# Attention scores of a head pair in two 64-row tiles of the array with three products, and probability transposes in halves of 64 queries

## The chip, the cores and the metric

The kernel runs on one core of a Trainium2 chip. The core has a matrix engine (TensorE, "PE" in the profile; its weight loads are listed apart as "PEld"), a vector engine (DVE), an activation engine (ACT), GpSimd (POOL), and a sync engine (SP) that here only issues transfers. Each engine takes its own queue of instructions in order; engines wait for one another through semaphores. Matrix results land in PSUM, where the kernel holds eight tiles ("banks") of 128 partitions by 512 fp32 numbers; all other on-chip data lies in SBUF. The metric is the device time of one execution in microseconds (us), the median of several runs.

A matrix instruction has a stationary operand, which is loaded into the array first (a weight load), and a moving operand, which is streamed through. The contraction runs over the partitions (the array's rows), and the columns of the stationary operand become the partitions of the result.

## The reference, cut to what matters

Two sequences (2048 and 512 tokens, 1024 channels, fp32) pass through an attention layer, a Fourier layer and a last norm. The change lies in the attention layer alone: 16 heads of 64 channels, 4 key/value heads, blocks of 128 queries that see three blocks of keys, an additive bias by distance, and a sink logit per head.

```python
h = rmsnorm(x, g)
z = h @ w_in                       # q, k, v, gate
scores = jnp.einsum('bnqhgd,bnkhd->bnhgqk', qb, kw).astype(jnp.float32) * scale + bias
scores = jnp.where(mask[None, :, None, None, :, :], scores, -jnp.inf)
m = jnp.maximum(jnp.max(scores, axis=-1, keepdims=True), sk)
p = jnp.exp(scores - m)
denom = jnp.sum(p, axis=-1, keepdims=True) + jnp.exp(sk - m)
p = p / denom
o = jnp.einsum('bnhgqk,bnkhd->bnqhgd', p, vw.astype(jnp.float32))
return x + (o * jax.nn.silu(gate)) @ w_out
```

## The kernel before

**Number format.** Products are made in `float32r`. Every operand is kept as two parts, `hi` (the number rounded to that type) and `lo` (the rest, made by DVE or POOL as number minus `hi`), and a product is the sum of hi·hi, hi·lo and lo·hi (`matmul3`, lines 93 to 97).

**Stages.** `attention_phase` goes through five chunks of 512 tokens (`CHUNKS`; chunk 0 is the short sequence, chunks 1 to 4 the long one). Each chunk projects keys and values (`kv_proj`), then runs 8 head pairs `p`, each with 4 query blocks `b` of 128 and 2 heads `j`. `fourier_phase` follows and is not touched.

**The loop.** For each chunk a loop over `i` (from 0 to 63 and a few more for the tail, line 712) has one (block, head) per step: `p, n = divmod(i, 8)`. A step traces, in this order: the scores of (b, j) (`at[p][1]`, line 742); the transposes of the probabilities that were scored `LAG` = 3 steps before (`at[..][2]`); half of this step's share of `fill`; every second step the product with the values, `av`, of the block whose transposes are `AVLAG` = 2 steps old, and after an odd block its `out_evac`; then the other half of `fill`. `fill` is the projection of the next head pair's queries and gates (`qg_proj`: 8 steps of three 512-column matmuls for q, an evacuation, the same for the gates), and for the last pair the output projection (`out_proj`), whose first half holds four PSUM banks at once (line 517).

**Scores (line 428).** `evac_q` (lines 370 to 378) writes, for each head, an operand of 128 rows: for head 0, `qa` has its 64 channels' hi in rows 0 to 63 (ACT, line 374) and their lo in rows 64 to 127 (DVE, line 375); for head 1, `qb` has hi in rows 64 to 127 (lines 376, 377) and lo in rows 0 to 63. The keys `kwin[g]` hold the same 64 channels twice, in rows 0 to 63 and again in rows 64 to 127, hi in part 0 and lo in part 1. So two matmuls of 128 rows per head, one with the keys' hi and one with their lo, give all four products. They go into one of two PSUM tiles `spt`, in turn. The moving operand has 384 columns (three blocks of keys), or 256 at either end of a sequence.

**Softmax.** On `S` (five buffers, `LAG + 2`): DVE adds the bias and takes the extremum (line 440), ACT takes the exponential and its sum (444), DVE the reciprocal (447) and the scaling (450; for chunk 0 and odd heads ACT, 453).

**Transposes (line 467).** Per (b, j) one transpose for each of the two or three blocks of keys; S is the stationary operand (128 queries by 128 keys), the identity the moving one (128 columns). The results of one head share a PSUM bank from the pool of six (`bank`); ACT writes hi (468) and DVE lo (469) into `pts`.

**Values (line 481).** Per block up to six matmuls of 256 columns (both heads side by side).

**Order.** The framework's scheduler places instructions by the order in which they are traced and by when its own model holds them ready; `tc.keep_in_program_order` pins an instruction behind all that was traced before it on its engine.

Of the kernel before, what the change touches and what calls it, by code (L numbers as in the profile page):

```python
# [18 lines left out]
P = 128  # L19
# [9 lines left out]
LAG = 3  # L29
AVLAG = 2  # L30
BIG = 1.0e30
LINE = 512
# [7 lines left out]
def f32(ap):  # L40
    return ap.bitcast(F32)
# [3 lines left out]
def encoder(  # L45
# [13 lines left out]
    ident = cpool.tile([P, P], F32, name="ident")  # L59
# [18 lines left out]
    def bank(name):  # L78
        return psum.tile([P, 512], F32, tag="bank", name=name)
# [55 lines left out]
    def attention_phase():  # L135

        with ExitStack() as es:
# [216 lines left out]
            def qg_proj(c, p, hs, res, invb=None):  # L354
# [15 lines left out]
                def evac_q():  # L370
                    ps = scaled(st["psq"], invb, f"q{p}")
                    qab = ap.tile([P, 2, CH], F32R, align_bytes=LINE, tag="qab", bufs=2, name=f"qab{c}_{p}")
                    qa, qb = qab[:, 0], qab[:, 1]
                    ACT.activation(qa[0:64], ps[0:64], AF.Copy, scale=-0.125)
                    DVE.scalar_tensor_tensor(qa[64:128], ps[0:64], -0.125, f32(qa[0:64]), ALU.mult, ALU.subtract)
                    ACT.activation(qb[64:128], ps[64:128], AF.Copy, scale=-0.125)
                    DVE.scalar_tensor_tensor(qb[0:64], ps[64:128], -0.125, f32(qb[64:128]), ALU.mult, ALU.subtract)  # L377
                    res["q"] = (qa, qb)
# [18 lines left out]
            def attention(c, p, res, uTs):  # L397
# [24 lines left out]
                def scores(b, j):  # L422
                    gb, k0, k1 = span(b)
                    q = res["q"][j][:, b * P : (b + 1) * P]
                    ps = spt[nS[0] % 2]
                    nS[0] += 1
                    for part in range(2):
                        PE.matmul(  # L428
                            ps[:, 2 + k0 * P : 2 + k1 * P],
                            q,  # L430
                            kwin[g][:, part, b * P + k0 * P : b * P + k1 * P],
                            start=part == 0,
                            stop=part == 1,
                        )
# [3 lines left out]
                    s = ap.tile([P, 388], F32, tag="S", bufs=LAG + 2, name=f"S{c}_{p}_{b}_{j}")  # L438
# [20 lines left out]
                def transp(b, j):  # L459
                    gb, k0, k1 = span(b)  # L460
                    s = st.pop((b, j))
                    if j == 0:
                        st["pt", b] = ap.tile([P, 2, 3, 2, P], F32R, align_bytes=LINE, tag="pt", bufs=2, name=f"pts{c}_{p}_{b}")
                    hi, lo = (st["pt", b][:, i] for i in range(2))
                    ps = bank(f"pt{c}_{p}_{b}_{j}").rearrange("p (k q) -> p k q", q=P)
                    for kb in range(k0, k1):
                        PE.transpose(ps[:, kb, :], s[:, 1 + kb * P : 1 + (kb + 1) * P], ident)  # L467
                    ACT.copy(hi[:, k0:k1, j, :], ps[:, k0:k1, :])  # L468
                    DVE.tensor_tensor(lo[:, k0:k1, j, :], ps[:, k0:k1, :], f32(hi[:, k0:k1, j, :]), ALU.subtract)  # L469
# [214 lines left out]
            HB = [(b, j) for b in range(4) for j in range(2)]  # L684
# [7 lines left out]
            for c in range(len(CHUNKS)):  # L692
# [19 lines left out]
                for i in range(64 + LAG + AVLAG):  # L712
# [851 lines left out]
```

## Time and profile before

| | |
|---|---|
| median of 3 runs | 1649.08 us (1646.85 to 1652.1) |
| the profiled execution's own time | 1648.75 us |
| its span from the first to the last instruction | 1647.0 us |
| mean granted TensorE clock | 0.998 |
| busy: PE, PEld, DVE, ACT, POOL | 99%, 85%, 73%, 54%, 26% |
| first and last score matmul (line 428) | 48.0 and 1071.8 us from the start of the span |
| score matmuls, transposes, value matmuls | 640, 896, 896 |

How to read it: the page and its views come from one profiled execution. In a timeline row the columns are the start in us, the length in us, the engine, the line of the kernel, the operation, what is written and read, and how many were merged into the row. The ends of matmuls are modelled, and neighbours overlap in the record: what a matmul occupies the array for is read from the starts of neighbours, not from the length. In a view of groups the columns are the line, engine, operation and form, the count, then the sum in us and the mean in ns, then idle time of that engine just before. A row of the view of stretches gives the stretch, its length, and for each engine its busy time and count of instructions.

### The profile page before, as it was taken

How to read it: one execution, taken by the hardware profiler on the slowest of the kernel's cores; microseconds unless marked ns; L12 is line 12 of the kernel's file. 1: busy time of each engine (PE TensorE's matmuls, PEld its weight loads, DVE VectorE, ACT ScalarE, POOL GpSimd, SP SyncE). 2: the span in 40 equal slices, each digit the busy share in tenths (PEclk: the TensorE clock that was granted, in tenths of full speed). 3: DMA queues.
4: the chain of work that ended last, by engine and by line, in shares of the span. 5: the costliest groups of instructions: out<-in, count | busy, mean ns of one | idle time of the engine just before them, and what ended most of it. 6: DMA issues, size and time to landing. Idle time of an engine off the chain costs nothing.

```text
span 1647.0 us, 25858 instructions
## 1 busy us (share of the span) xinstructions
PE 1628.4 (99%) x8939; PEld 1401.4 (85%) x8939; DVE 1199.0 (73%) x2844; ACT 892.7 (54%) x2035; POOL 434.5 (26%) x605
## 2 busy tenths in 40 slices
PE   9999999999999999999999999999999999999998
PEld 7887888888898888988888888888888888888886
DVE  6787565888538886478884588858767667988696
ACT  6788644677326675256762466636545454343252
POOL 2454751431404322224214142121111111100010
PEclk9999999999999999999999999999999999999999
DMA  8475886665766555765648765657565469655862
GB/s 303 150 284 213 314 319 225 221 230 186 278 218 227 196 217 182 279 250 160 233 140 312 252 210 187 217 195 249 205 237 185 173 220 391 217 192 191 333 208 90
DMA packets 100637, 374.05 MB, mean 227 GB/s; under 512 B 12139, under 2 KB 22379, under 8 KB 83100
## 3 DMA queue, kind: packets, MB, share of 16 engines
q1 hardware_dynamic: 81708, 297.91, 52.2%
q0 software_dynamic: 16464, 70.30, 11.0%
q10 hardware_dynamic: 2336, 4.20, 0.7%
q8 instruction: 71, 1.16, 0.3%
q14 instruction: 58, 0.48, 0.1%
HBM read 281.10 MB, written 91.26 MB: 226 GB/s over the span
## 4 chain that ended last, share of the span: by engine, by line
PE 82%; DMA 4%; DVE 4%; POOL 3%; ACT 3%; issue 2%; SPq 0%; POOLq 0%; DVEq 0%; ACTq 0%
PE av L481 6%; PE spt L428 6%; PE pt L467 5%; PE qp L95 4%; PE qp L97 4%; PE qp L96 4%; PE op L95 4%; PE gp L95 4%; PE op L97 4%; PE gp L97 4%; PE op L96 4%; PE gp L96 4%; PE W L96 2%; PE W L97 2%; PE W L95 2%
## 5 line engine op out<-in xcount | busy, mean ns | idle before, releaser
L444 ACT ACTIVATE S<-S 128x385 f32<-128x385 f32 (+1 forms) x320 | 190.8, 596 | 63.3 <-DVE S L440 61.5
L469 DVE TENSOR_TENSOR pts<-pt,pts 128x384 fp32r<-128x384 f32 (+1 forms) x320 | 168.4, 526 | 42.0 <-ACT pts L468 39.6
L468 ACT CAST pts<-pt 128x384 fp32r<-128x384 f32 (+1 forms) x320 | 144.0, 452 | 83.4 <-PE pt L467 80.3
L440 DVE CUSTOM_DVE_ANT_0 S<-spt,b 128x385 f32<-128x385 f32 (+1 forms) x320 | 168.4, 527 | 28.2 <-PE spt L428 25.7
L428 PE MATMUL spt<-kwin,qab 128*128 128x384 f32 (+1 forms) x640 | 157.2, 327 | 1.9 <-DVE S L440 1.7
L500 POOL TENSOR_TENSOR o<-o,s 128x256 f32<-128x256 f32 x75 | 55.3, 738 | 375.0 <-DVE o L498 374.9
L467 PE MATMUL pt<-ident,S 128*128 128x128 f32 x896 | 150.7, 273 | 0.0
L428 PEld LDWEIGHTS spt<-kwin,qab 128*128 128x128 f32 x640 | 117.9, 188 | 27.9 <-DVE S L440 3.0
L95 PE MATMUL qp<-h,wq 128*128 128x512 f32 x320 | 137.5, 430 | 2.0 <-ACT wq L116 1.4
L95 PE MATMUL gp<-h,wg 128*128 128x512 f32 x320 | 137.8, 431 | 0.0
L481 PEld LDWEIGHTS av<-pts,v 128*128 128x128 f32 x896 | 126.3, 189 | 12.1 <-DVE qab L377 0.6
L481 PE MATMUL av<-pts,v 128*128 128x256 f32 x896 | 135.8, 285 | 0.3 <-DVE qab L377 0.2
L95 PE MATMUL op<-wo,uT 128*128 128x512 f32 x320 | 126.5, 397 | 1.6 <-ACT invb L173 0.9
L97 PE MATMUL qp<-h,wq 128*128 128x512 f32 x320 | 126.7, 396 | 0.2 <-POOL wq L121 0.2
L467 PEld LDWEIGHTS pt<-ident,S 128*128 128x128 f32 x896 | 113.9, 140 | 15.1 <-DVE pts L469 3.5
L96 PE MATMUL qp<-h,wq 128*128 128x512 f32 x320 | 126.2, 395 | 0.0
L97 PE MATMUL gp<-h,wg 128*128 128x512 f32 x320 | 125.9, 393 | 0.0
L96 PE MATMUL gp<-h,wg 128*128 128x512 f32 x320 | 125.7, 393 | 0.0
L96 PE MATMUL op<-wo,uT 128*128 128x512 f32 x320 | 125.7, 393 | 0.0
L97 PE MATMUL op<-wo,uT 128*128 128x512 f32 x320 | 124.7, 391 | 0.0
L450 DVE TENSOR_SCALAR S<-S 128x384 f32<-128x384 f32 (+1 forms) x256 | 118.7, 464 | 7.9
L447 DVE RECIPROCAL S<-S 128x1 f32<-128x1 f32 x320 | 51.3, 160 | 65.7 <-ACT S L444 62.7
(408 smaller groups left out, 4252.4 us busy)
## 6 DMA issues: line engine op xcount, KB each, us to landing
wo<-wsd SPq DMA_DIRECT2D x32, 1024.0 KB, 5.0
wq<-wsd SPq DMA_DIRECT2D x31, 1024.0 KB, 4.9
wg<-wsd SPq DMA_DIRECT2D x31, 1024.0 KB, 6.8
x<-x1d SPq DMA_DIRECT2D x40, 512.0 KB, 3.9
b<-b21d SPq DMA_DIRECT2D x40, 512.0 KB, 5.4
b<-rowd SPq DMA_DIRECT2D x40, 384.0 KB, 4.3
xs<-in_x_dram SPq DMA_DIRECT2D x23, 512.0 KB, 6.1
s2d<-gt POOLq DMA_DIRECT2D x40, 256.0 KB, 3.9
```

Of the source, the lines that this page charges most:

```text
L95: PE.matmul(out, a[0], b[0], start=start, stop=False, skip_group_check=more)
L96: PE.matmul(out, a[0], b[1], start=False, stop=False, skip_group_check=more)
L97: PE.matmul(out, a[1], b[0], start=False, stop=stop, skip_group_check=more)
L428: PE.matmul(ps[:, 2 + k0 * P : 2 + k1 * P], q, kwin[g][:, part, b * P + k0 * P : b * P + k1 * P], start=part == 0, stop=part == 1,)
L440: DVE.tensor_tensor_reduce(out=s[:, e0:e1], in0=ps[:, 1 + e0 : 1 + e1], in1=st["bias"][:, j, 386 - e1 : 386 - e0][:, ::-1], scale=1.0, sca ...
L444: last_exp[0] = ACT.activation(s[:, e0:e1], s[:, e0:e1], AF.Exp, bias=mn, scale=-1.0, accum_out=den)
L450: DVE.tensor_scalar(s[:, ks], s[:, ks], den, None, ALU.mult)
L467: PE.transpose(ps[:, kb, :], s[:, 1 + kb * P : 1 + (kb + 1) * P], ident)
L468: ACT.copy(hi[:, k0:k1, j, :], ps[:, k0:k1, :])
L469: DVE.tensor_tensor(lo[:, k0:k1, j, :], ps[:, k0:k1, :], f32(hi[:, k0:k1, j, :]), ALU.subtract)
L481: PE.matmul(out, v, pt[:, kb].rearrange("p h q -> p (h q)"), start=kb == k0 and part == 0, stop=kb == k1 - 1 and part == 1,)
L500: eng.tensor_tensor(o, o, s, ALU.mult)
```

## The change

One head of a pair now lives in rows 0 to 63 of the array and the other in rows 64 to 127, so that every score matmul and every transpose has 64 rows; instructions of the two halves are issued in turn, pinned in program order.

- `evac_q`: one ACT and one DVE instruction over 128 partitions write hi and lo of both heads; `qab` now has hi in `[:, 0]` and lo in `[:, 1]`, each head in its own 64 rows.
- `scores(b)` does both heads of a block: three products (hi·hi, hi·lo, lo·hi) for each, that is six matmuls of 64 rows; head j goes to `spt[j]`. `soft(b, j)` is the softmax as it was.
- `transp(b)` does both heads of a block: for each head and block of keys two transposes, of queries 0 to 63 (rows 0 to 63 of S, into one PSUM bank) and of queries 64 to 127 (rows 64 to 127, into another); 12 where there were 6. Then one hi and one lo instruction per half of the queries.
- The loop: every second step (even `i`) traces the transposes first, of the block scored `LAG` = 4 steps before, then the scores; `av` comes 2 steps after the transposes, as before. `S` keeps five buffers.

```diff
-LAG = 3
+LAG = 4
...
-                    qa, qb = qab[:, 0], qab[:, 1]
-                    ACT.activation(qa[0:64], ps[0:64], AF.Copy, scale=-0.125)
-                    DVE.scalar_tensor_tensor(qa[64:128], ps[0:64], -0.125, f32(qa[0:64]), ALU.mult, ALU.subtract)
-                    ACT.activation(qb[64:128], ps[64:128], AF.Copy, scale=-0.125)
-                    DVE.scalar_tensor_tensor(qb[0:64], ps[64:128], -0.125, f32(qb[64:128]), ALU.mult, ALU.subtract)
-                    res["q"] = (qa, qb)
+                    ACT.activation(qab[:, 0], ps, AF.Copy, scale=-0.125)
+                    DVE.scalar_tensor_tensor(qab[:, 1], ps, -0.125, f32(qab[:, 0]), ALU.mult, ALU.subtract)
+                    res["q"] = qab
...
-                def scores(b, j):
+                def scores(b):
                     gb, k0, k1 = span(b)
-                    q = res["q"][j][:, b * P : (b + 1) * P]
-                    ps = spt[nS[0] % 2]
-                    nS[0] += 1
-                    for part in range(2):
-                        PE.matmul(
-                            ps[:, 2 + k0 * P : 2 + k1 * P],
-                            q,
-                            kwin[g][:, part, b * P + k0 * P : b * P + k1 * P],
-                            start=part == 0,
-                            stop=part == 1,
-                        )
+                    for i, (qp, kp) in enumerate(((0, 0), (0, 1), (1, 0))):
+                        for j in range(2):
+                            rows = slice(64 * j, 64 * j + 64)
+                            tc.keep_in_program_order(PE.matmul(
+                                spt[j][:, 2 + k0 * P : 2 + k1 * P],
+                                res["q"][rows, qp, b * P : (b + 1) * P],
+                                kwin[g][rows, kp, b * P + k0 * P : b * P + k1 * P],
+                                start=i == 0,
+                                stop=i == 2,
+                            ))
+                    for j in range(2):
+                        soft(b, j)
+
+                def soft(b, j):
+                    gb, k0, k1 = span(b)
+                    ps = spt[j]
...
-                    s = ap.tile([P, 388], F32, tag="S", bufs=LAG + 2, name=f"S{c}_{p}_{b}_{j}")
+                    s = ap.tile([P, 388], F32, tag="S", bufs=5, name=f"S{c}_{p}_{b}_{j}")
...
-                def transp(b, j):
+                def transp(b):
                     gb, k0, k1 = span(b)
...
-                    for kb in range(k0, k1):
-                        PE.transpose(ps[:, kb, :], s[:, 1 + kb * P : 1 + (kb + 1) * P], ident)
-                    ACT.copy(hi[:, k0:k1, j, :], ps[:, k0:k1, :])
-                    DVE.tensor_tensor(lo[:, k0:k1, j, :], ps[:, k0:k1, :], f32(hi[:, k0:k1, j, :]), ALU.subtract)
+                    ps = [bank(f"pt{c}_{p}_{b}_{h}")[:, :384].rearrange("p (k j q) -> p k j q", k=3, j=2) for h in range(2)]
+                    for j in range(2):
+                        for kb in range(k0, k1):
+                            for h in range(2):
+                                rows = slice(64 * h, 64 * h + 64)
+                                tc.keep_in_program_order(
+                                    PE.transpose(
+                                        ps[h][:, kb, j, :], ss[j][rows, 1 + kb * P : 1 + (kb + 1) * P], ident[rows, rows]
+                                    )
+                                )
+                    for h in range(2):
+                        hi, lo = (pts[:, i, k0:k1, :, 64 * h : 64 * h + 64] for i in range(2))
+                        ACT.copy(hi, ps[h][:, k0:k1])
+                        DVE.tensor_tensor(lo, ps[h][:, k0:k1], f32(hi), ALU.subtract)
...
-                    if i < 64:
-                        at[p][1](*HB[n])
                     k = i - LAG
-                    if 0 <= k < 64:
-                        at[k // 8][2](*HB[k % 8])
+                    if 0 <= k < 64 and k % 2 == 0:
+                        at[k // 8][2](k % 8 // 2)
+                    if i < 64 and n % 2 == 0:
+                        at[p][1](n // 2)
...
-                    if 0 <= k < 64 and k % 2 == 1:
+                    if 0 <= k < 64 and k % 2 == 0:
```

More of the change, by code (lines that the diff above doesn't have):

```diff
@@ L457, in scores @@
                     st[b, j] = s
-                def transp(b, j):
+                def transp(b):
                     gb, k0, k1 = span(b)
[L461 to L465, printed above, removed]
-                    for kb in range(k0, k1):
-                        PE.transpose(ps[:, kb, :], s[:, 1 + kb * P : 1 + (kb + 1) * P], ident)
-                    ACT.copy(hi[:, k0:k1, j, :], ps[:, k0:k1, :])
-                    DVE.tensor_tensor(lo[:, k0:k1, j, :], ps[:, k0:k1, :], f32(hi[:, k0:k1, j, :]), ALU.subtract)
+                    ss = [st.pop((b, j)) for j in range(2)]
+                    pts = ap.tile([P, 2, 3, 2, P], F32R, align_bytes=LINE, tag="pt", bufs=2, name=f"pts{c}_{p}_{b}")
+                    st["pt", b] = pts
+                    ps = [bank(f"pt{c}_{p}_{b}_{h}")[:, :384].rearrange("p (k j q) -> p k j q", k=3, j=2) for h in range(2)]
[12 more added lines that the diff above has]
+                        DVE.tensor_tensor(lo, ps[h][:, k0:k1], f32(hi), ALU.subtract)
                 def av(b):
@@ L683, in attention_phase @@
             AHEAD = ahead()
-            HB = [(b, j) for b in range(4) for j in range(2)]
             tail = []
```

## The prediction

> **What bounds the kernel now.** I read the page first (busy shares, chain of waits), then the view of waits for PE, then the busy time by stretches.
>
> ```profile
> span 1647.0 us, 25858 instructions
> PE 1628.4 (99%) x8939; PEld 1401.4 (85%) x8939; DVE 1199.0 (73%) x2844; ACT 892.7 (54%) x2035; POOL 434.5 (26%) x605
> PE 82%; DMA 4%; DVE 4%; POOL 3%; ACT 3%; issue 2%; SPq 0%; POOLq 0%; DVEq 0%; ACTq 0%
> ...
> PE spt L428 <- DVE S L440: 1.7, 2, 1.4
> ...
> 45.00:210.00 165.00, 159.67 (x882) 134.94 (x881) 122.00 (x411) 127.58 (x311) 93.55 (x134) 0.99 0.67 242
> 870.00:1090.00 220.00, 220.00 (x1224) 191.45 (x1223) 149.06 (x424) 111.03 (x278) 61.79 (x84) 1.00 0.67 235
> ```
>
> PE carries the span: 82% of the chain is PE, and its longest wait in total is 1.7 us. In the last chunk's stretch (870 to 1090) PE is busy for the whole 220 us, DVE for 149. Only in chunk 0's stretch (45 to 210) is PE idle, 165.00 - 159.67 = 5.3 us. So the time of the attention stage is the sum of what PE's instructions occupy, and the change is priced in PE time. Busy is not full use, so I go to the timeline of single instructions, one head's scores and transposes first.
>
> ```profile
> 365.02 0.40 PE L97 MATMUL qp<-h,wq 128*128 128x512 f32 x1
> 365.25 0.51 PE L428 MATMUL spt<-kwin,qab 128*128 128x384 f32 x2
> 365.43 0.42 PEld L467 LDWEIGHTS pt<-ident,S 128*128 128x128 f32 x3
> 365.61 0.49 PE L467 MATMUL pt<-ident,S 128*128 128x128 f32 x3
> 365.82 0.19 PEld L95 LDWEIGHTS qp<-h,wq 128*128 128x128 f32 x1
> 365.85 0.47 PE L95 MATMUL qp<-h,wq 128*128 128x512 f32 x1
> 365.93 0.19 PEld L96 LDWEIGHTS qp<-h,wq 128*128 128x128 f32 x1
> 366.16 0.39 PE L96 MATMUL qp<-h,wq 128*128 128x512 f32 x1
> ...
> 360.62 0.40 PE L428 MATMUL spt<-kwin,qab 128*128 128x256 f32 x2
> 360.86 0.49 PE L467 MATMUL pt<-ident,S 128*128 128x128 f32 x3
> ...
> 370.02 0.51 PE L428 MATMUL spt<-kwin,qab 128*128 128x384 f32 x2
> 370.37 0.38 PE L467 MATMUL pt<-ident,S 128*128 128x128 f32 x2
> 370.51 0.48 PE L95 MATMUL gp<-h,wg 128*128 128x512 f32 x1
> 370.82 0.40 PE L96 MATMUL gp<-h,wg 128*128 128x512 f32 x1
> ```
>
> A 512-column matmul takes 365.25 - 365.02 = 0.23 us. Two score matmuls of 384 columns take 365.61 - 365.25 = 0.36 us, **0.18** each; two of 256 columns 360.86 - 360.62 = 0.24, **0.12** each. From the first of three transposes to L96 it is 366.16 - 365.61 = 0.55; less the 0.23 of L95 that leaves 0.32 us, **0.107** per transpose; two take 370.82 - 370.37 - 0.23 = 0.22. A transpose streams only 128 columns, a third of a score matmul's, and takes more than half its time. The reason is in the PEld rows: L95's load starts at 365.82 and the next one, L96's, at 365.93, 0.11 us later, although PE's record has L95 started at 365.85. A load of 128 columns takes about 0.11, it starts when the matmul before takes over the weights loaded earlier, and a transpose is too short to hide the next load. Transposes are bound by their loads; score matmuls hide theirs.
>
> **The change part by part.** How many blocks there are:
>
> ```profile
> L428 PE MATMUL spt<-kwin,qab 128*128 128x384 f32 x512 | 131.5, 338 | 1.7 <-DVE S L440 1.7
> L428 PE MATMUL spt<-kwin,qab 128*128 128x256 f32 x128 | 25.7, 283 | 0.1
> L467 PE MATMUL pt<-ident,S 128*128 128x128 f32 x896 | 150.7, 273 | 0.0
> ```
>
> Four score matmuls make a block of a head pair: 512/4 = 128 full blocks and 128/4 = 32 at an end (check: 128 x 6 + 32 x 4 = 896 transposes). PE time of one now: full, 2 x (0.36 + 0.32) = 1.36 us; end, 2 x (0.24 + 0.22) = 0.92 us.
>
> *Scores.* Six matmuls of 64 rows replace four of 128. If the two heads' matmuls run at the same time in their halves of the array, a pair costs one row's 0.18: 3 x 0.18 = 0.54 instead of 0.72 (end 0.36 instead of 0.48). If they do not overlap, 6 x 0.18 = 1.08. No instruction of the trace shares the array with another, so the bounds of a pair are 0.18 and 0.36. I take 0.18: the heads use other rows, other operands and separate banks. The Trainium skill ("TensorE: Matmul & The Clock Gate", Part 3, Measured speedup vs the span model) says that tiles in different rows run together and that each further one adds some 4 ns; by it the three pairs would cost 0.55. No run here shows that yet.
>
> *Transposes.* 12 of 64 rows and 64 columns replace 6. Their stationary operand still has 128 columns. If both halves load at the same time, 6 pairs x 0.107 = 0.64, as before; if one load follows the other, 12 x 0.107 = 1.28. The streamed half (64 columns in place of 128) saves nothing, because the load decides. I take the pair, as for the scores; one assumption serves both. So **with pairs side by side** a full block costs 0.54 + 0.64 = 1.18, 0.18 less; an end 0.36 + 4 x 0.11 = 0.80, 0.12 less. In all -128 x 0.18 - 32 x 0.12 = **-26.9 us**.
>
> *Going to 64 rows and back.* Twice per block PE now passes between matmuls of the full array and of half of it. The trace has one place with a smaller tile, the bias row product at line 245 (33 rows, 16 columns):
>
> ```profile
> 17.47 0.39 PE L97 MATMUL kp<-h,wk 128*128 128x512 f32 x1
> 17.79 0.11 PEld L245 LDWEIGHTS bp<-oh,rb 33*16 33x16 f32 x2 [0.35 <-issue]
> 17.79 1.03 PE L245 MATMUL bp<-oh,rb 33*16 33x512 f32 x2
> 18.75 0.19 PEld L95 LDWEIGHTS vp<-wv,h 128*128 128x128 f32 x1 [0.85 <-ACT xs L155]
> 18.86 0.19 PEld L96 LDWEIGHTS vp<-wv,h 128*128 128x128 f32 x1
> ```
>
> On the way in: L97's columns are through at 17.47 + 0.23 = 17.70; elsewhere the next load would have started with L97 at 17.47, here it starts at 17.79 and names no releaser ("issue"). That is 0.09 us of empty array, and a load of 128 columns in place of these 16 would add 0.11: 0.20. On the way out: L245's last matmul ends on record at 18.82; in the rows above a matmul starts 0.17 before the recorded end of the one ahead (365.25 against 365.42), so the next was due at 18.65. L95 could not stream before its weights were in, at 18.86, when L96's load starts: 0.21, unless ACT, which the row names, held some of it. It is not the plain fp32 of line 245 that makes the gap, since the transposes are plain fp32 too and their load starts at 365.43, together with the second score matmul. I take **0.40 us for a round trip**, 160 times: **+64 us**. The bounds are 0 (as between scores and transposes now) and 0.5.
>
> The Trainium skill ("TensorEngine Tiling (Array Packing)", Tiling Modes, Key Properties) says that changing the tiling mode, not merely the tile, drains TensorE. The two gaps at line 245 agree with it; by that rule the 0.40 is paid, without it the sum would be the -26.9 alone.
>
> *Softmax and the lag.* The work is the same, but both heads' scores now arrive together every second step, and the transposes come 4 steps after in place of 3.
>
> ```profile
> L444 ACT ACTIVATE S<-S 128x385 f32<-128x385 f32 (+1 forms) x320 | 190.8, 596 | 63.3 <-DVE S L440 61.5
> L440 DVE CUSTOM_DVE_ANT_0 S<-spt,b 128x385 f32<-128x385 f32 (+1 forms) x320 | 168.4, 527 | 28.2 <-PE spt L428 25.7
> L450 DVE TENSOR_SCALAR S<-S 128x384 f32<-128x384 f32 (+1 forms) x256 | 118.7, 464 | 7.9
> ```
>
> One head's chain is about 0.53 + 0.60 + 0.46, with the short reads some 2 us, so 4 us for both in a row. The scores at 360.62 and at 370.02 are four steps apart: 9.4 us. The chain is hidden, also with 5 buffers, since a pair of transposes frees its two just ahead. Cost 0; without that cover it would be 4 us per block.
>
> *Evacuations.* hi and lo of `pts` keep their counts and element numbers (two ACT and two DVE instructions per block). For q two of four instructions go:
>
> ```profile
> L374 ACT ACTIVATE qab<-qp 64x512 fp32r<-64x512 f32 x40 | 23.4, 584 | 12.5 <-PE qp L97 7.8 <-DVE qp L270 4.5
> L375 DVE SCALAR_TENSOR_TENSOR qab<-qp,qab 64x512 fp32r<-64x512 f32 x40 | 27.4, 684 | 14.8 <-ACT qab L374 13.9
> ```
>
> 23 us of ACT and 27 of DVE, on engines that do not bound. Only chunk 0 can turn them into time, at most its 5.3 us of PE idle: 0 to -5, I take -2.
>
> *Banks.* The pool has six. In the last head pair the output projection holds four, `av` one, and the transposes now want two at once: one too many. They must then wait for `out_evac`:
>
> ```profile
> 362.97 0.58 ACT L489 COPY t<-av 64x512 f32<-64x512 f32 x1
> 363.73 0.84 DVE L498 TENSOR_TENSOR o<-av,t 64x256 f32<-64x256 f32 x2
> ```
>
> 0.58 + 0.84 = 1.4 us, twice per chunk, five chunks: at most 14 us. Queued behind the pinned transposes are the pinned scores of the next block and so its softmax; output projection matmuls (12 x 0.23 = 2.8 us a step) can be placed ahead and cover it. 0 to +14, I take +2. This and the -2 cancel.
>
> **Sum**: -26.9 + 64 - 2 + 2 = +37 us. The profiled execution took 1648.75 us (span 1647.0), which is the median of the runs shown, 1649.08, within 0.4. 1649.1 + 37 = **1686 us**, slower by 2.2%.
>
> **The rivals.**
>
> *No price for the passage* (it ends on the other side). If a pair of half rows needs no emptying of the array, the -26.9 stands alone: 1622 us. Place: the 320 passages between lines 97, 467 and 428. It decides where a round trip costs under 26.9/160 = 0.17 us. For it: the trace's only passage is of another shape, few rows and few columns, one single time, and its way out may be a wait for ACT. Against it: both gaps are there, of the same size. At 0.17 the change would be no change.
>
> *Loads one after another.* If matmuls pair up but only one weight load runs at a time, transposes cost 1.28 and the scores are bound by six loads, 6 x 0.11 = 0.66: 1.94 a full block, 0.58 more; an end 8 x 0.11 + 0.66 = 1.54, 0.62 more: 128 x 0.58 + 32 x 0.62 = +94 us, 1743; with the passages +158, 1807. For it: the trace has no two loads at once, and a load is what transposes wait for. Against it: they use other rows.
>
> *The halves don't run side by side at all*: 1.28 + 1.08 = 2.36, 1.00 more (end 0.88 + 0.72, 0.68 more): 128 + 22 = +150, with the passages +214, 1863 us.
>
> **How the numbers follow.** Forecast (pairs, passages paid) 0.38, with its own range 1665 to 1715 (a round trip of 0.3 to 0.5, the banks' 14). No price for the passage 0.29. A round trip near 0.17, no change, 0.05. Loads one after another 0.08 at 1743 and 0.13 at 1807. Not side by side 0.07. The range runs from 1612 (1622 less chunk 0's 5, and as much for my readings) to 1755 (1743 and the banks): it holds the first four, 0.80. A change of 0.3%, 5 us, is about what a measurement of this kernel can tell from none. Faster 0.29, same 0.05, slower 0.66.
>
> **What would show it.** In the timeline after: pairs of score rows 0.18 apart per product, not 0.36; loads of both halves that start together or 0.11 apart; 12 transposes in 0.64 or in 1.28; a load at the start of each block of transposes that starts with the matmul before (no price) or 0.3 after it. What would make the forecast wrong: PE no longer busy throughout in the stretch of the last chunk, with waits for DVE or for banks, since I hold the rest of the stage to be covered by PE.

## The result, and the profile after

The changed kernel takes 1692.28 us (median of 4 runs, 1688.87 to 1696.69) against 1648.64 us of the kernel before on the same chip: ratio 1.0261, 95% interval 1.0244 to 1.0277. It is slower by 44 us; the forecast was 37 slower, with a range of 1612 to 1755. The profiled execution took 1692.7 us.

The page of after, with the lines that answer to those of before (span, busy shares, chain of waits):

```profile
span 1690.8 us, 28290 instructions
PE 1654.4 (98%) x10155; PEld 1341.7 (79%) x10155; DVE 1171.3 (69%) x2804; ACT 863.1 (51%) x1995; POOL 435.0 (26%) x605
PE 56%; DVE 15%; issue 9%; ACT 7%; POOL 6%; DMA 6%; SPq 0%; POOLq 0%; DVEq 0%; ACTq 0%
```

PE is still busy for 98%, yet its share of the chain fell from 82% to 56%, and DVE's rose from 4% to 15%: the kernel is no longer bound by PE alone. To see where, the span is cut at the first score matmul of each chunk (in after 0.8 us ahead of it) and at the first Fourier product (view of stretches; first before, then after; the columns are as in the prediction).

```profile
48.00:270.10 222.10, 216.65 (x1200) 184.80 (x1199) 153.34 (x457) 149.51 (x353) 109.28 (x151) 0.99 0.71 256
270.10:487.70 217.60, 217.60 (x1232) 190.30 (x1231) 154.64 (x443) 119.47 (x304) 61.86 (x77) 1.00 0.64 225
487.70:710.80 223.10, 223.10 (x1264) 195.28 (x1263) 160.32 (x443) 123.50 (x304) 62.12 (x77) 1.00 0.63 220
710.80:927.70 216.90, 216.90 (x1213) 189.22 (x1212) 153.36 (x426) 117.26 (x283) 61.35 (x80) 1.00 0.64 225
927.70:1113.10 185.40, 185.27 (x1026) 159.55 (x1024) 143.29 (x416) 110.14 (x276) 52.43 (x75) 1.00 0.60 207
```

```profile
48.00:277.60 229.60, 221.56 (x1424) 175.16 (x1424) 153.07 (x449) 145.44 (x345) 109.89 (x152) 0.99 0.68 248
277.60:507.20 229.60, 224.41 (x1473) 179.06 (x1472) 148.16 (x435) 113.47 (x296) 61.75 (x77) 1.00 0.61 214
507.20:741.00 233.80, 230.20 (x1520) 182.97 (x1519) 152.74 (x435) 116.82 (x296) 61.80 (x77) 1.00 0.60 210
741.00:969.10 228.10, 223.88 (x1470) 176.91 (x1469) 147.06 (x418) 110.67 (x275) 61.53 (x80) 1.00 0.60 214
969.10:1157.10 188.00, 186.60 (x1268) 145.77 (x1266) 136.51 (x409) 104.28 (x269) 52.69 (x75) 1.00 0.59 203
```

Chunks 0 to 3 grew by 7 to 12 us each, the last one by under 3, and the phase after 1113.1 (now 1157.1) not at all: 533.9 us before, 533.7 after. In chunks 1 to 3, where PE showed no idle time, it now idles 5.2, 3.6 and 4.2 us. That is under half of the growth, so PE's own work is longer too, or is held up where the record shows one long matmul.

The views of waits, after (engine, line, what is waited for: us in total, times, longest) and the same DVE row of before:

```profile
DVE pts L481 <- ACT pts L480: 107.8, 92, 3.7
...
PE spt L425 <- DVE S L443: 8.0, 16, 1.0
PE av L493 <- DVE pts L481: 4.9, 9, 0.9
```

```profile
DVE pts L469 <- ACT pts L468: 39.6, 42, 3.3
```

Score matmuls wait for DVE to have read their PSUM tile (line 443), 8.0 us on record where it was 1.7; and DVE waits 108 us instead of 40 for ACT's hi of the transposes. One such place in the timeline of after, chunk 1 (rows left out are other work):

```profile
337.37 0.59 PE L474 MATMUL pt<-ident,S 64*128 64x64 f32 x12
...
337.76 0.77 PE L425 MATMUL spt<-kwin,qab 64*128 64x384 f32 x6
...
339.91 0.74 POOL L512 TENSOR_TENSOR o<-o,s 128x256 f32<-128x256 f32 x1 [5.75 <-DVE o L510]
...
340.68 0.41 ACT L513 CAST uT<-o 128x256 fp32r<-128x256 f32 x1 [1.74 <-POOL o L512]
...
341.11 0.86 ACT L480 CAST pts<-pt 128x384 fp32r<-128x384 f32 x2
...
341.63 1.02 DVE L481 TENSOR_TENSOR pts<-pt,pts 128x384 fp32r<-128x384 f32 x2 [1.80 <-ACT pts L480]
...
342.13 0.47 PE L474 MATMUL pt<-ident,S 64*128 64x64 f32 x8
...
342.57 0.55 DVE L443 CUSTOM_DVE_ANT_0 S<-spt,b 128x385 f32<-128x385 f32 x1
...
343.18 1.27 PE L425 MATMUL spt<-kwin,qab 64*128 64x384 f32 x6 [0.58 <-DVE S L443]
```

The transposes of 337.37 ended before 338, but their hi (L480) is written only at 341.11, behind `uT` (L513), which stood 1.74 us waiting for POOL (L512). DVE's lo (L481) waits for that hi, and behind lo in DVE's queue stand the reads (L443) of the scores of 337.76, from 342.57 on. Only they free `spt` for the scores of 343.18, which stand in PE's queue with the product matmuls behind them. The six scores that took 0.77 now take 1.27 on record: the view of busy time hides half of this stop.

Now a visit to the 64-row mode without a stop; PE and PEld of after in two stretches, one with scores alone and one with transposes and scores at the end of a sequence:

```profile
969.53 0.39 PE L97 MATMUL gp<-h,wg 128*128 128x512 f32 x1
969.85 0.79 PE L425 MATMUL spt<-kwin,qab 64*128 64x384 f32 x6
...
969.85 0.47 PEld L425 LDWEIGHTS spt<-kwin,qab 64*128 64x128 f32 x6 [0.35 <-issue]
970.56 0.19 PEld L95 LDWEIGHTS qp<-h,wq 128*128 128x128 f32 x1 [0.25 <-PE spt L425]
970.67 0.19 PEld L96 LDWEIGHTS qp<-h,wq 128*128 128x128 f32 x1
...
980.89 0.39 PE L97 MATMUL gp<-h,wg 128*128 128x512 f32 x1
981.21 0.59 PE L474 MATMUL pt<-ident,S 64*128 64x64 f32 x12
...
981.57 0.43 PEld L425 LDWEIGHTS spt<-kwin,qab 64*128 64x128 f32 x6
982.14 0.19 PEld L95 LDWEIGHTS gp<-h,wg 128*128 128x128 f32 x1
982.25 0.19 PEld L96 LDWEIGHTS gp<-h,wg 128*128 128x128 f32 x1
```

L97's columns are through at 969.53 + 0.23 = 969.76. The scores' load starts at 969.85 (0.09 empty) and takes 0.11: 0.20 on the way in, as in the forecast. On the way out L95 can stream at 970.67, when L96's load starts. Three pairs at 0.168 (the starts of single records) end at 969.96 + 0.50 = 970.46: 0.21, as in the forecast. With transposes first, the way in is 0.09 and a load of 0.06. The twelve transposes stand between 981.21 and the scores' load at 981.57. The forecast's 0.107 per pair would be 0.64 for a full block; the starts of single records give **0.063** per pair, 0.38. The two halves of a pair start 3 to 7 ns apart.

From the starts of all PE instructions between the first score and the first Fourier product I made a ledger in us. A matmul counts from its recorded start, or from the end of its weight load where that is later (0.11 us after the load began, 0.06 for a transpose). A passage is the interval between two such starts across a change of mode, less the time of the first one's columns; a stop is an interval more than 0.06 us longer than the columns take. The transposes include 41 that are not of probabilities; e1 and e9 are experiments below.

| | before | after | e1 | e9 |
|---|---|---|---|---|
| matmuls of the full array, without transposes | 851.0 | 859.4 | 848.1 | 846.8 |
| scores and transposes | 214.1 | 182.3 | 154.3 | 149.9 |
| of these, stops inside a visit | | 27.6 | 6.2 | |
| passages (visits to 64 rows) | 0 | 67.6 (181) | 69.9 (189) | 64.2 (176) |
| sum | 1065.1 | 1109.3 | 1072.3 | 1060.9 |

So before to after is +67.6 for passages, +27.6 for stops, +8.4 in the full array's stretches, and -59.4 for the rest of scores and transposes (182.3 - 27.6 - 214.1): +44.2. The rows are good to some 2 us and the sums to 1 us. Before has about 6 us of stops of its own among the 214.1, nearly all in chunk 0, so the pairs alone save some 53 us here (and some 60 in e9, below).

### The profile page after: what moved, and what is told of

It reads as the page before. It is cut to its first block, busy times and chain, and to the rows that moved or that the text cites. A ratio compares the mean times of both kernels' runs of the same rounds, so it can differ in the third digit from the quotient of the medians.

```text
span 1690.8 us, 28290 instructions
## 1 busy us (share of the span) xinstructions
PE 1654.4 (98%) x10155; PEld 1341.7 (79%) x10155; DVE 1171.3 (69%) x2804; ACT 863.1 (51%) x1995; POOL 435.0 (26%) x605
## 4 chain that ended last, share of the span: by engine, by line
PE 56%; DVE 15%; issue 9%; ACT 7%; POOL 6%; DMA 6%; SPq 0%; POOLq 0%; DVEq 0%; ACTq 0%
DVE pts L481 3%; PE op L97 3%; PE op L96 3%; PE op L95 3%; PE av L493 3%; ACT S L447 2%; DVE S L443 2%; PE fo L96 2%; PE fo L97 2%; PE qp L95 2%; PE fo L95 2%; PE spt L425 2%; POOL o L512 2%; PE qp L96 2%; PE qp L97 2%
## 5 line engine op out<-in xcount | busy, mean ns | idle before, releaser
L481 DVE TENSOR_TENSOR pts<-pt,pts 128x384 fp32r<-128x384 f32 (+1 forms) x320 | 157.0, 525 | 109.1 <-ACT pts L480 107.8
L443 DVE CUSTOM_DVE_ANT_0 S<-spt,b 128x385 f32<-128x385 f32 (+1 forms) x320 | 158.3, 525 | 5.1 <-PE spt L425 5.0
L512 POOL TENSOR_TENSOR o<-o,s 128x256 f32<-128x256 f32 x75 | 55.7, 743 | 405.4 <-DVE o L510 387.3
L425 PE MATMUL spt<-kwin,qab 64*128 64x384 f32 (+1 forms) x960 | 138.5, 358 | 9.3 <-DVE S L443 8.0
L480 ACT CAST pts<-pt 128x384 fp32r<-128x384 f32 (+1 forms) x320 | 132.6, 458 | 21.4 <-PE pt L474 19.6
L95 PE MATMUL qp<-h,wq 128*128 128x512 f32 x320 | 133.5, 417 | 3.3 <-ACT wq L116 2.8
L95 PE MATMUL gp<-h,wg 128*128 128x512 f32 x320 | 133.0, 416 | 0.0
L95 PE MATMUL op<-wo,uT 128*128 128x512 f32 x320 | 127.5, 400 | 1.7 <-ACT invb L173 1.3
L97 PE MATMUL op<-wo,uT 128*128 128x512 f32 x320 | 125.5, 394 | 1.3 <-DVE uT L514 1.3
L96 PE MATMUL op<-wo,uT 128*128 128x512 f32 x320 | 126.5, 395 | 0.0
L97 PE MATMUL qp<-h,wq 128*128 128x512 f32 x320 | 126.2, 394 | 0.1
L96 PE MATMUL qp<-h,wq 128*128 128x512 f32 x320 | 126.2, 394 | 0.0
L96 PE MATMUL gp<-h,wg 128*128 128x512 f32 x320 | 125.8, 393 | 0.0
L97 PE MATMUL gp<-h,wg 128*128 128x512 f32 x320 | 125.0, 391 | 0.0
L474 PEld LDWEIGHTS pt<-ident,S 64*128 64x128 f32 x1792 | 70.4, 138 | 62.6 <-issue 40.5
L425 PEld LDWEIGHTS spt<-kwin,qab 64*128 64x128 f32 x960 | 86.0, 187 | 24.5 <-DVE S L443 18.6
L474 PE MATMUL pt<-ident,S 64*128 64x64 f32 x1792 | 94.3, 232 | 2.0 <-DVE o L510 1.3
L95 PEld LDWEIGHTS qp<-h,wq 128*128 128x128 f32 x320 | 60.3, 188 | 27.2 <-issue 10.4
```

The lines of the kernel that those rows point to most:

```text
L95: PE.matmul(out, a[0], b[0], start=start, stop=False, skip_group_check=more)
L96: PE.matmul(out, a[0], b[1], start=False, stop=False, skip_group_check=more)
L97: PE.matmul(out, a[1], b[0], start=False, stop=stop, skip_group_check=more)
L425: tc.keep_in_program_order(PE.matmul(spt[j][:, 2 + k0 * P : 2 + k1 * P], res["q"][rows, qp, b * P : (b + 1) * P], kwin[g][rows, kp, b * P ...
L443: DVE.tensor_tensor_reduce(out=s[:, e0:e1], in0=ps[:, 1 + e0 : 1 + e1], in1=st["bias"][:, j, 386 - e1 : 386 - e0][:, ::-1], scale=1.0, sca ...
L474: PE.transpose(ps[h][:, kb, j, :], ss[j][rows, 1 + kb * P : 1 + (kb + 1) * P], ident[rows, rows])
```

## The experiments

**e1_soft_first: the scores' softmax ahead of the transposes' evacuation.** The theory was that the stops come from the traced order alone. The edit gives DVE the reads of `spt` first, pins lo behind them, and traces ACT's hi behind the softmax; the matmuls are the same, and PE's order changes a little (189 visits to 64 rows in place of 181).

```diff
-                        at[k // 8][2](k % 8 // 2)
+                        evac = at[k // 8][2](k % 8 // 2)
                     if i < 64 and n % 2 == 0:
                         at[p][1](n // 2)
+                    if evac:
+                        evac()
...
-                        DVE.tensor_tensor(lo, ps[h][:, k0:k1], f32(hi), ALU.subtract)
+                            lo = DVE.tensor_tensor(lo, ps[h][:, k0:k1], f32(hi), ALU.subtract)
+                            after(lo, last_red[0])
```

> The changed kernel with another order on ACT and DVE: the evacuation of the transposes (hi by ACT, lo by DVE) is traced behind the softmax of the scores that follow them, and the lo instructions are queued behind the two bias instructions that read spt; the matmuls are the same. Theory (queue order): the profile of the changed kernel has 27.6 us of stops inside the 64-row visits, nearly all before or between score matmuls that wait for DVE to read spt, because that read is queued behind lo instructions that wait for ACT. With the read ahead of them these stops should be under 5 us and the time 1692 - 23 to 28 = 1664 to 1669 us, and a few us more if the order makes more visits (189 in place of 181 by its order, 8 x 0.4 = +3). Rival (banks, or ACT simply too slow): the time stays within 5 us of 1692.

Measured: 1657.9 us, ratio 1.0049 (1.0032 to 1.0067), 34 us less than after and below the 1664 to 1669 expected. Its stretches of chunks 1 to 3 and its waits:

```profile
276.30:494.40 218.10, 217.77 (x1472) 175.83 (x1471) 140.30 (x435) 113.72 (x296) 62.55 (x77) 1.00 0.65 225
494.40:717.10 222.70, 222.37 (x1521) 179.47 (x1520) 145.58 (x435) 117.75 (x296) 62.57 (x77) 1.00 0.64 220
717.10:933.60 216.50, 216.18 (x1471) 173.45 (x1470) 138.50 (x418) 111.39 (x275) 61.74 (x80) 1.00 0.65 225
...
PE pt L475 <- DVE s L383: 5.1, 2, 2.6
...
DVE pts L484 <- ACT pts L483: 24.6, 13, 3.7
```

Chunks 1 to 3 are level with before (217.6, 223.1, 216.9), and PE is idle for 0.33 us in each. The stops fell from 27.6 to 6.2 us, all in chunk 0, where transposes wait twice for a bank that DVE frees (L383). The order on ACT and DVE was the cause, and it cost more than I had sized it: the full array's stretches came down by 11 us with it. The move of hi and the pin of lo were not tried apart.

**e2_double_passage: the price of a passage.** On top of e1, a step of three full-array products stands between the transposes and the scores, so that most visits become two (317 for 189).

```diff
-        PE.matmul(out, a[0], b[0], start=start, stop=False, skip_group_check=more)
+        first = PE.matmul(out, a[0], b[0], start=start, stop=False, skip_group_check=more)
+        if pin[0]:
+            tc.keep_in_program_order(first)
...
-                    if i < 64 and n % 2 == 0:
-                        at[p][1](n // 2)
...
+                        pin[0] = n % 2 == 0
                         for s in todo[: m // 2]:
                             s()
+                        pin[0] = False
+                    if i < 64 and n % 2 == 0:
+                        at[p][1](n // 2)
+                    if evac:
+                        evac()
```

> As e1_soft_first, with a full-array step of three matmuls of the projection moved in between the transposes and the scores of most visits, so that PE passes to 64 rows and back 317 times in place of 189; the work is the same. Theory (each passage empties the array and shows one load, 0.36 to 0.40 us a round trip by the profile of the changed kernel): 128 x 0.38 = +49 us against e1_soft_first, 45 to 52. Rival (passages are free or cost only what the loads of transposes cost anyway): 0 to +10 us. Rival (the forecast's reading from line 245 holds as a whole only by luck, a passage costs half): +25 us.

Measured: 1693.02 us, ratio 1.0265 (1.0248 to 1.0282), 35 us over e1, where 45 to 52 were expected. One pair of visits in its timeline (PE):

```profile
967.02 0.59 PE L479 MATMUL pt<-ident,S 64*128 64x64 f32 x12
967.54 0.50 PE L97 MATMUL gp<-h,wg 128*128 128x512 f32 x1
...
968.43 0.79 PE L430 MATMUL spt<-kwin,qab 64*128 64x384 f32 x6
969.15 0.50 PE L97 MATMUL gp<-h,wg 128*128 128x512 f32 x1
```

By the ledger passages cost 119.4 us for 317 visits, 0.377 each, against 69.9 / 189 = 0.370 in e1: the price is as theorised. What I had overlooked is on the other side: scores and transposes fell by 13 us (154.3 to 141.4). Some 5 us of it is the load of the first scores behind transposes, which e1 pays inside the visit (0.04 us in most visits), and some 6 us the stops of e1 in chunk 0, which e2 does not have. So an added visit cost 35 / 128 = 0.27 us net, or 0.32 with those stops counted out.

**e3_full_transposes: what halving the transposes is worth.** On top of e1 the transposes are whole again (128 rows, 128 columns, six per block); the scores stay in 64 rows, and the passages too.

```diff
                         for kb in range(k0, k1):
-                            for h in range(2):
-                                rows = slice(64 * h, 64 * h + 64)
-                                        ps[h][:, kb, j, :], ss[j][rows, 1 + kb * P : 1 + (kb + 1) * P], ident[rows, rows]
+                                PE.transpose(ps[j][:, kb, :], ss[j][:, 1 + kb * P : 1 + (kb + 1) * P], ident)
```

> As e1_soft_first, but the transposes are whole again (128 queries, 128 columns, full array), beside scores that stay in pairs of 64 rows: about 162 round trips in place of 189. Theory (a plain fp32 transpose is bound by its 128 streamed columns, 0.109 us, and a pair of half transposes takes 0.063): a full block's transposes go from 0.38 to 0.65 us and an end's from 0.25 to 0.44, 128 x 0.27 + 32 x 0.19 = +41 us, less 27 x 0.38 = 10 for the passages: +31 us against e1_soft_first. Rival (the forecast's reading: the load of 128 columns bounds a transpose, so halves in pairs bring nothing): -10 us.

Measured: 1685.56 us, ratio 1.0223 (1.0206 to 1.024), 28 us over e1. In its timeline (PE, PEld):

```profile
967.65 0.82 PE L473 MATMUL pt<-ident,S 128*128 128x128 f32 x6
...
968.39 0.42 PEld L426 LDWEIGHTS spt<-kwin,qab 64*128 64x128 f32 x6 [0.17 <-DVE S L451]
```

Six whole transposes take 0.74 us to the next load (that is 6 x 0.107, and 0.10 that I take for the emptying; the row names a wait for DVE, which may hold some of it), where twelve halves take 0.36 to 0.40. By the ledger scores and transposes rose by 33.4 us (187.7 for 154.3), and 28 visits fewer gave back 5.4. Had transposes been bound by their loads, halving them would be worth nothing. What bounds the halves is open: their 0.063 is more than half of 0.107 and close to the 0.06 of a load.

**e4_heads_in_turn: does the alternating order make the pairs?** On top of e1 the scores are issued three of head 0, then three of head 1.

```diff
-                    for i, (qp, kp) in enumerate(((0, 0), (0, 1), (1, 0))):
-                        for j in range(2):
+                    for j in range(2):
+                        for i, (qp, kp) in enumerate(((0, 0), (0, 1), (1, 0))):
```

> As e1_soft_first, but the score matmuls are issued head by head (three of head 0, then three of head 1) in place of head 0 and head 1 in turn. Theory (matmuls start in the order of issue, so only neighbours in other rows run together): one pair overlaps in place of three, 5 x 0.167 in place of 3 x 0.167 for a full block, +0.33 us, an end +0.23: 128 x 0.33 + 32 x 0.23 = +50 us against e1_soft_first. Rival (the two halves of the array run on by themselves, whatever the order): within 5 us of e1_soft_first.

Measured: 1655.01 us, ratio 1.0038 (1.0026 to 1.0051), 3 us under e1. My theory fell. First e4's row and the load that ends its visit, then those of e1:

```profile
966.35 0.77 PE L426 MATMUL spt<-kwin,qab 64*128 64x384 f32 x6
...
967.05 0.19 PEld L95 LDWEIGHTS qp<-h,wq 128*128 128x128 f32 x1 [0.25 <-issue]
```

```profile
968.44 0.77 PE L426 MATMUL spt<-kwin,qab 64*128 64x384 f32 x6
969.14 0.50 PE L95 MATMUL qp<-h,wq 128*128 128x512 f32 x1
```

Both visits last 0.70 us from their first score to L95; one after another, six would take 6 x 0.168 = 1.01 before anything empties. In e4's single records the scores start at 966.348 and 966.351, 966.608 and 966.611, 966.783 and 966.786: still in pairs, the fourth instruction of the order beside the first. The Trainium skill ("TensorE: Matmul & The Clock Gate", Part 3, The mechanism) says that matmuls start and end strictly in program order; for two row halves this run shows otherwise, and the measurement decides. The 3 us lie in chunk 0: from first score to first score it takes 224.3 us for 228.4 in e1, and the other four chunks together take 2.2 us more.

**e5_before_order: the order's fault in the kernel before.** The kernel before, with the transposes traced ahead of the scores and the read of `spt` queued behind lo, as the change has it; no 64-row tiles.

```diff
+                    after(red, last_pts[0])
...
-                    if i < 64:
-                        at[p][1](*HB[n])
...
+                    if i < 64:
+                        at[p][1](*HB[n])
```

> The kernel before, with full-array scores and transposes, and only the order changed: in each step the transposes are traced ahead of the scores, and the bias instruction that reads spt is queued on DVE behind the lo instruction of those transposes. Theory (the queue order alone makes the stops, whatever the array does): PE waits for DVE to read spt, +10 to +35 us against the kernel before, 1659 to 1684 us, with waits of score matmuls for DVE in the profile. Rival (the order hurts only together with both heads at once, where a block's two reads stand behind two lo instructions): within 5 us of the kernel before.

Measured: 1667.38 us, ratio 1.0111 (1.0093 to 1.0129), 18 us slower than before, with no passage at all; stops between full matmuls rose from 12.6 to 32.6 us. The order costs time by itself, but only in part where after lost it: from first score to first score chunk 0 takes 234.1 us for 222.1, and chunks 1 to 3 together 664.3 for 657.6, 6.7 us more, where after lost 33.9 and e1 got them back. In its view of waits, score matmuls wait for DVE only 2.5 us. In chunks 1 to 3, then, the order hurts mainly together with both heads at once, which is near to the rival; what makes the 12 us in chunk 0 was not tried.

**e6_banks and e9_banks_all: the banks of the last head pair.** On top of e1, in the last head pair `av` and `out_evac` of odd blocks come ahead of the transposes, which are ordered behind them (e6). After has 150 visits with both transposes and scores, 11 of scores alone and 20 of transposes alone. Of these 31, the first two score blocks and the last two transpose blocks of each chunk make 20, since with a lag of 4 steps they have no partner; the other 11 are splits, 10 of them single transposes of head pair 7. In e1 there are 18 such single transposes.

```diff
+                    early_av = 56 < i and 0 <= kA < 64 and kA % 4 == 2
+                    if early_av:
+                        at[kA // 8][3](kA % 8 // 2)
+                        free = at[kA // 8][4](kA % 8 // 2)
                     if 0 <= k < 64 and k % 2 == 0:
-                        evac = at[k // 8][2](k % 8 // 2)
+                        evac = at[k // 8][2](k % 8 // 2, free)
...
+                                if free is not None:
+                                    after(t, free)
+                                    free = None
```

> As e1_soft_first, but in the last head pair of each chunk, while the output projection holds four banks, the value product of an odd block and its evacuation are traced ahead of the transposes, and these are ordered behind the evacuation, so that both banks are free when they start. By its order 181 visits in place of 190: the single transposes that the scheduler had issued alone, with full-array matmuls behind them, go from 18 to 9. Theory (each such split costs a passage): 9 x 0.38 = 3.4 us less than e1_soft_first, about 1654. Rival (the bank shortage is hidden, the splits fill a wait that now shows): within 2 us of e1_soft_first or slower.

Measured for e6: 1653.49 us, ratio 1.0024 (1.0013 to 1.0035), 4.4 us under e1 with 180 visits for 189. The two ran on different chips; by their ratios to the kernel before it is 0.25%, 4.1 us. The waits of transposes for `out_evac` (DVE's `o`), 1.4 us in eight places in e1, are 0.3 us in one.

e9 has e7's edit (below) too, and one more, which is not what its expectation says: no further `av` is moved. In the even blocks of the last head pair the first transpose is ordered behind the scaling of the softmax that was traced two steps before.

```diff
-                        DVE.tensor_scalar(s[:, ks], s[:, ks], den, None, ALU.mult)
+                        last_scl[0] = DVE.tensor_scalar(s[:, ks], s[:, ks], den, None, ALU.mult)
...
+                            last_lo2[0] = last_scl[0] if h else last_lo2[0]
...
+                    if i > 56 and not early_av:
+                        free = last_lo2[0]
```

> The best run so far (softmax of the scores ahead of the transposes' evacuation, banks of the last head pair kept free in odd blocks, chunk 0's copies on ACT), with the values' product put ahead of the transposes in every block of the last head pair where it was not yet, so that a few single transposes that were issued alone join their group again. Theory, a visit to the 64-row mode costs 0.37 to 0.40 us: some 4 visits fewer, 1.5 us faster, 1643 to 1645 us. Rival, the visits that are left are not held by banks: no change, 1645.5 us within 1.

Measured for e9: 1642.96 us, ratio 0.9964 (0.9952 to 0.9976), 2.5 us under e7 with 176 visits for 180. The intervals of e7's and e9's ratios overlap slightly and the chips differ, so the gain is likely and not certain. In e6 a missing bank showed mostly as split visits and little as a wait. In e9 four single transposes joined their groups because the first one was held back, so that banks had held these four is not shown.

**e7_banks_copies and e8_before_copies: two small copies of chunk 0.** On top of e6, the two copies of the sink column, which chunk 0 makes on DVE per head pair, go to ACT, as in a run of its own on the kernel before.

```diff
-                    DVE.tensor_copy(bt[:, :, 0], sk[:, 2 * p : 2 * p + 2])
-                    DVE.tensor_copy(bt[:, :, 385], sk[:, 2 * p : 2 * p + 2])
+                    for e in (0, 385):
+                        (DVE.tensor_copy if c else ACT.copy)(bt[:, :, e], sk[:, 2 * p : 2 * p + 2])
```

> As e6_banks, and in chunk 0 the two small bias edge copies of each head pair go from DVE to ACT. In e1_soft_first two of them took 3.85 and 1.93 us on DVE beside POOL's weight splits, and PE stood 2.7 us at transposes right behind, twice. Theory (the DVE queue behind these copies held a bank): 5 us less than e6_banks, about 1649, level with the kernel before (1648.8). Rival (POOL and DVE block each other anyway and the next DVE instruction takes the delay): within 2 us of e6_banks.

Measured for e7: 1645.47 us, ratio 0.9985 (0.9974 to 0.9996), 8 us under e6 by the medians. The profiled executions are only 4.6 us apart, as that of e6 was its fastest; chunk 0 alone is 5.5 us shorter. The wait of transposes for L383, which e1 had, is gone.

> The kernel before with one edit: the two small copies of the sink column into the bias tile, which chunk 0 makes on DVE in each head pair, go to ACT as in the other chunks. It is the control to the run that ended 0.15% below the kernel before and had that edit too. Theory: in the kernel before those copies hold nothing that the matrix engine waits for (the longest of them takes 0.66 us there), so the time stays within 2 us of 1648.6 us, and the run with the changed kernel owes its 8 us to copies that had become long and late in the changed kernel's order. Rival: the edit helps any order of chunk 0, since the kernel before has 5.3 us of idle matrix engine in that chunk; then this run is 3 to 5 us faster than the kernel before (1643.5 to 1645.5 us), and the changed arrangement has no gain of its own over it.

Measured for e8: 1651.67 us, ratio 1.0018 (1.0009 to 1.0027): 2.7 us slower than the kernel before, a little more than the 2 us allowed for, and not faster. The copies had become long only in the changed order (at worst 0.8 us in before, 3.4 in after and 3.9 in e1), and the kernel before has nothing to gain from that edit, so e9's lead does not come from it. The orders of e6 and e9 were not tried on the kernel before, which has 12.6 us of stops of its own; whether they would help it too is open. The page of e9, the fastest kernel here:

```profile
span 1640.9 us, 28398 instructions
PE 1623.8 (99%) x10155; PEld 1328.8 (81%) x10155; DVE 1135.3 (69%) x2788; ACT 865.4 (53%) x2011; POOL 437.0 (27%) x605
PE 89%; DVE 4%; ACT 2%; DMA 2%; issue 2%; POOL 1%; DVEq 0%; POOLq 0%; SPq 0%; ACTq 0%
```

PE is the chain again. In the ledger scores and transposes take 64.2 us less than before (214.1 - 149.9) and the passages cost 64.2. Some 4 us of the saving is stops (6 in before, 2 left in e9), so the pairs alone, some 60 us, do not quite pay for the passages. The lead of 6 us over the kernel before comes from stops that are gone, from the full array's stretches (846.8 for 851.0) and small rests.

## Why the prediction was right or wrong

The sign and, within 6 us, the time were right, but the closeness is luck: two errors cancel. Transposes saved far more than I took them to, and the order of the queues cost about as much, which I had put at nothing.

- *Passages, +64 forecast: right.* 0.373 us for a round trip (67.6 / 181) against 0.40, and e2, with 128 visits more, paid 0.377. The rivals "no price for the passage" and "round trip 0.17" fall. The count was off, 181 instead of 160: the lag leaves two blocks of scores and two of transposes in each chunk without a partner (+10), and 11 visits were split. The Trainium skill's rule ("TensorEngine Tiling (Array Packing)", Tiling Modes, Key Properties) that a change of mode drains TensorE agrees with this trace; the 0.37 is the runs' figure for it.
- *Scores, a pair at 0.18: right* (0.168). The rivals with loads one after another or no overlap fall; halves start within 4 ns.
- *Transposes: wrong.* The step that failed is "Transposes are bound by their loads", and with it 0.107 for a pair and no gain. The trace of before has the answer where single loads are read: PEld of before at a place where the array stood empty, first from a narrow stretch with one load in it, then from a wider one:

```profile
51.49 0.14 PEld L467 LDWEIGHTS pt<-ident,S 128*128 128x128 f32 x1 [0.45 <-ACT qab L376]
...
51.49 0.20 PEld L467 LDWEIGHTS pt<-ident,S 128*128 128x128 f32 x2 [0.45 <-ACT qab L376]
51.66 0.19 PEld L95 LDWEIGHTS gp<-h,wg 128*128 128x128 f32 x1
```

One load is 0.14 long on record, two together 0.20: the second starts 0.06 after the first, as soon as nothing streams. L95's starts 0.11 after the second, when the first transpose's 128 columns are through. A load of plain fp32 takes 0.06, and the 0.107 is the stream of 128 columns of plain fp32. Half as many columns take 0.063, so the pairs saved 53 us (59 with before's own stops) and not 27; e3 shows 28 to 33 us of it to hang on the halving.
- *Softmax and the lag, "Cost 0": wrong.* I costed the chain by its durations (4 us under a cover of 9.4) and not by the place of its first instruction in DVE's queue. The change traces the transposes' evacuation ahead of the scores' softmax, so the read of `spt` stands behind lo, lo behind hi, hi behind `uT`, and `uT` behind POOL. I looked for what waits behind the moved instructions on PE, and not on DVE and ACT. e1 took 34 us away by the order alone; e5 put 18 into the kernel before, though 12 of them in chunk 0.
- *Banks, +2: mechanism right, its form wrong.* I priced a wait of transposes for `out_evac`. In after it is 1.3 us in eight places; the rest appears as split visits, and e6, which frees the banks, is 4.4 us faster than e1.
- *Evacuations, -2: not seen.* Chunk 0's idle PE went from 5.45 us (222.10 - 216.65) to 8.04 (229.60 - 221.56). The order alone does not explain it, as in e1 it is 10.33 (228.30 - 217.97); there the small copies held it, which e7 moved.
- *What would make the forecast wrong* was stated for the last chunk, as its sign of a failing cover. There PE idles 1.4 us, and it is the chunk that grew least; the sign appeared in chunks 1 to 3. The trace of after gives a likely reason: in DVE's order of the last chunk 25 of 64 reads of `spt` stand alone between two lo instructions, in chunks 1 to 3 only 2, 8 and 6, where nearly every pair of reads stands behind both. No run tries this by itself.

## What to carry to other kernels

Before an instruction is moved, follow each queue that its consumers stand in: a DVE queue that waits for ACT, which waits for POOL, stopped PE here although the durations of the softmax were well covered. Price a smaller array tile by visits: each costs about 0.37 us in this kernel (0.27 to 0.32 net where e2 split one), so collect all work of one tile size in one visit, and see to the banks that would split it. And where a stream and a weight load could both explain a spacing, look for a place where the array was empty: there the load stands alone.

## What the runs showed of the hardware that was not expected

- The two row halves of the array run on from their own instructions: issued three and three (e4), the matmuls still start in pairs 3 ns apart.
- A weight load of 128 columns takes 0.06 us for a transpose of plain fp32 and 0.11 for float32r (982.14 to 982.25 above, into an empty array), and 128 columns of plain fp32 stream for about 0.11 us, where 256 columns of float32r take 0.12.
- DVE's copy of two columns took 0.15 us in the median of e1 and 3.85 us at worst, with a splitting of weights on POOL running beside it. That the one holds up the other was not tried by itself.
